# Weights and activations of a split-precision decoder step, laid out with equal addresses modulo 256 bytes

## Chip, cores and metric

The kernel runs on one core of one Trainium2 chip. The metric is the device time of one execution in microseconds; of the kernel before there are three, with a median of 1106.64 us.

## What is computed

One layer of a hybrid decoder trunk, for a prompt of 256 tokens and for 8 sequences of 4 new tokens, 288 tokens in all. `D_MODEL` is 2048, `D_FF` 8192, all arrays float32. Cut to what matters:

```python
h = rmsnorm(x, norm1_g)
proj = einsum("btd,de->bte", h, w_in) + b_in          # 2048 -> 3072
a, gate, z = split(proj)                              # 1024 each
u = a * sigmoid(gate)
c = silu(layernorm(depthwise_causal_conv(u_ext, conv_w, conv_b), ln_g, ln_b))
d = multiscale_pool(z_ext, pos0)                      # windows 2, 4, 8, 16
p = einsum("btgc,gce->btge", d, pool_w) * pool_scale
x = x + einsum("btm,md->btd", concat([c, p]), w_out)  # 2048 -> 2048
f = square(relu(einsum("btd,df->btf", rmsnorm(x, norm2_g), w_ff1)))
x = x + einsum("btf,fd->btd", f, w_ff2)
y = rmsnorm(x, norm_f)
```

## The kernel before

**Products in three parts.** Channels lie on the partitions and the 288 tokens on the free axis. A product of float32 matrices is made of three matmuls in the type float32r: every operand is split into a high part (a rounded copy) and a low part (what the rounding left), and `gemm` (L283 to L301) adds high weights by high activations (L297), high weights by low activations (L298) and low weights by high activations (L299) into one bank of PSUM. A matmul is 128 channels by 128 outputs by 288 tokens. `gemm` goes over k, the tiles of 128 input channels, and within each k over m, the two output tiles of 128; so six matmuls belong to one k. All matrices together make 8112 of them: 3072 each for `w_ff1` and `w_ff2`, 768 for `w_out`, 1152 for `w_in`, 48 for the pool weights.

**Weights.** They come in blocks of 1024 x 256 (`load`, L153), as two raw tiles of four k by 256 columns, on SP's DMA queue. `split` (L273) takes two tiles for each raw tile from the pool `wspl` (`spl`, L267: `whi` and `wlo`, five buffers of each), and `split_part` (L251) fills them in one of three ways, by the table `WAYS`: ACT always makes the high part (L257); the low part comes from DVE (way V, L262), from POOL in two halves (way G, L265), or, in way D, ACT writes the negative of the high part (L259) and a DMA on POOL's queue adds the raw weights to it (L260). The feed-forward weights all go way V. `columns` (L270) gives the slices of one k and m.

**Activations.** `act2` (L117) gives one tile for two k: `[P, 2, 2, T]`, with the low part in slot 0 and the high part in slot 1 of each k. `hx` (the first norm), `dx` (pooling), `mx` (convolution group), `ax` (second norm) and `fx` (feed-forward) are made so. For `ax`, the groups 4 and 5 lie in the place of `z_all` (L563 to L565), the groups 6 and 7 in tiles of the tag `c` (L567 to L571).

**Addresses.** A slot of an activation tile is 288 x 4 = 1152 bytes, 4.5 x 256. All tiles of weights and activations start at 128 modulo 256 bytes, and their sizes are multiples of 256. So, modulo 256: weights, high and low, are read from 128 for every k and m; high activations from 128 + 1152, that is 0; low activations from 128.

**Order.** A scheduler places the instructions of each engine by the time at which it expects them; the convolution's work is put back by `later`. The order of the groups is written out in `SEQUENCE`: eight convolution pairs and four pool groups with the first layer's weights, then eight groups of `w_out` for the pool half and eight for the convolution half, with the layer norm between them (`ln_mean`, L506), then four rounds of eight groups of `w_ff1` and eight of `w_ff2`. TensorE takes the products in this order; the scheduler can interleave neighbours.

Of the kernel before, what the change touches and what calls it, by code (L numbers as in the profile page):

```python
# [10 lines left out]
F32R = mybir.dt.float32r  # L11
AF = mybir.ActivationFunctionType
ALU = mybir.AluOpType
# [3 lines left out]
P = 128  # L17
# [3 lines left out]
T = SEQ + NB * NS  # L21
# [62 lines left out]
def trunk_kernel(ctx: ExitStack, tc: tile.TileContext, io):  # L84
# [3 lines left out]
    nc = tc.nc  # L88
# [4 lines left out]
    wspl = ctx.enter_context(tc.tile_pool(name="wspl", bufs=5))  # L93
    actp = ctx.enter_context(tc.tile_pool(name="actp", bufs=8))
# [8 lines left out]
    def nm(s):  # L103
        seen[s] = seen.get(s, 0) + 1
        return f"{s}{seen[s]}"
# [11 lines left out]
    def act2(name, **kw):  # L117

        t = actp.tile([P, 2, 2, T], F32R, name=nm(name), **(kw or {"tag": "act"}))
        return t[:, :, 1, :], t[:, :, 0, :]  # L120

    def tmp(name, n=T, tag="tmp", bufs=2):
        return tmpp.tile([P, n], F32, name=nm(name), tag=tag, bufs=bufs)
# [4 lines left out]
    def f32(t):  # L128
        return t.bitcast(F32)
# [41 lines left out]
    def by_pair(t):  # L171
        return t[:].rearrange("p (i k) c -> p i k c", i=2)
# [76 lines left out]
    turns = {}  # L249

    def split_part(raw, src, hi, lo, way):  # L251

        nc.scalar.copy(hi, raw)  # L257
        if way == "D":
            nc.scalar.activation(lo, f32(hi), AF.Copy, scale=-1.0)  # L259
            nc.gpsimd.dma_start(lo, src, accum_op=ALU.add)  # L260
        elif way == "V":
            nc.vector.tensor_tensor(lo, raw, f32(hi), op=ALU.subtract)  # L262
        else:
            for j in range(0, raw.shape[1], 2):
                nc.gpsimd.tensor_tensor(lo[:, j : j + 2, :], raw[:, j : j + 2, :], f32(hi[:, j : j + 2, :]), op=ALU.subtract)  # L265

    def spl():  # L267
        return [wspl.tile([P, 4, 256], F32R, name=nm("w" + part), tag="w" + part) for part in ("hi", "lo")]

    def columns(hi, lo, k, m):  # L270
        return hi[:, k, m * P : (m + 1) * P], lo[:, k, m * P : (m + 1) * P]

    def split(halves, stage="ff"):  # L273

        parts = []
        for raw, src in halves:
            turns[stage] = turns.get(stage, -1) + 1
            parts.append(spl())
            ways = WAYS.get(stage) or WAYS[stage[0]]
            split_part(raw, src, *parts[-1], ways[turns[stage] % len(ways)])  # L280
        return lambda k, m: columns(*parts[k // 4], k % 4, m)

    def gemm(banks, rhs, m_outer=False, between={}):  # L283
# [25 lines left out]
    def halves(x2):  # L309

        return [(x2[0][:, m, :], x2[1][:, m, :]) for m in range(2)]


    hx, firsts = [], []

    def first_split(k0, n):
        for k in range(k0, k0 + n):
            if k % 2 == 0:
                hx.extend(halves(act2("hx")))
            hh, hl = hx[k]  # L320
            nc.scalar.activation(hh, xT[:, k, :], AF.Copy, scale=v("norm1_g", k))
            nc.vector.scalar_tensor_tensor(out=hl, in0=xT[:, k, :], scalar=v("norm1_g", k), in1=f32(hh), op0=ALU.mult, op1=ALU.subtract)
        if k0 % 2 == 0:
            firsts.append([by_pair(t) for t in spl()])
        at = slice(k0 % 2, k0 % 2 + n)
        raw, hi, lo = (t[:, :, at, :] for t in (raws[k0 // 2], *firsts[k0 // 2]))
        split_part(raw, None, hi, lo, "V")
# [9 lines left out]

    def pool_weights(g):
        raw, (hi, lo) = load_pool(g), spl()
        split_part(raw[:, 0:2, :], None, hi[:, 0:2, :], lo[:, 0:2, :], "V")  # L340
        return lambda k, m: columns(hi, lo, k, m)

    def weight_groups():
# [197 lines left out]
    for j, c in enumerate(cs):  # L541
        n = tmpp.tile([P, 2, T], F32, name=nm("n"), tag="ag", bufs=2)
        nc.vector.tensor_tensor(n, c, norm["rows"][:, None, :].to_broadcast([P, 2, T]), op=ALU.mult)
        for m in range(2):
            i = 2 * j + m
# [9 lines left out]
    for g in range(8):  # L555
        bk = bank2()
        gemm(each(bk), mixc)
        x2 = xT[:, 2 * g : 2 * g + 2, :]
        nc.vector.tensor_tensor(x2, x2, bk[:, :, :T], op=ALU.add)
        if g < 4:  # L560
            a2 = halves(act2("ax", tag="p", bufs=4))
        elif g < 6:
            if g == 4:  # L563
                ax45 = zp.tile([P, N8 * ZL], F32R, name="ax45", tag="z")
                ax45 = ax45[:, 32 : 32 + 8 * T].rearrange("p (g m q t) -> p g m q t", g=2, m=2, q=2)  # L565
            a2 = halves((ax45[:, g - 4, :, 1, :], ax45[:, g - 4, :, 0, :]))
        else:  # L567
            a2 = []
            for m in range(2):
                t2 = actp.tile([P, 2, T], F32R, name=nm("ax"), tag="c", bufs=4)  # L570
                a2.append((t2[:, 1, :], t2[:, 0, :]))  # L571
        for m, (ah, al) in enumerate(a2):
            k = 2 * g + m
            xk = xT[:, k, :]
            nc.scalar.activation(ah, xk, AF.Copy, scale=v("norm2_g", k))
            nc.vector.scalar_tensor_tensor(out=al, in0=xk, scalar=v("norm2_g", k), in1=f32(ah), op0=ALU.mult, op1=ALU.subtract)
            x1.append((ah, al))
            if k == 0:
                nc.scalar.activation(ss2, xk, AF.Square)
            else:  # L580
                q2 = tmp("q")
                nc.scalar.activation(q2, xk, AF.Square)
                nc.gpsimd.tensor_tensor(ss2, ss2, q2, op=ALU.add)
# [107 lines left out]
```

## Time and profile before

| what | us |
|---|---|
| runs: median (lowest, highest) | 1106.64 (1105.6, 1106.66) |
| profiled execution: span from first to last instruction | 1103.1 |
| PE busy | 1087.3 (99%) |
| DVE busy | 638.2 (58%) |
| ACT busy | 477.8 (43%) |
| POOL busy | 179.1 (16%) |

Of the profiled execution only the span is given; the runs' median is 3.5 us above it. PE is TensorE's matmul row and PEld its weight loads, which overlap it; DVE, ACT and POOL are VectorE, ScalarE and GpSimd; SP issues most of the DMAs. Matmuls are pipelined: each takes some 290 ns from start to end, and the next starts long before that, so their rate is read from their starts. In a row of instructions the name after the line is the output tile, then the inputs, without buffer numbers.

### The profile page before, as it was taken

The page shows a single profiled execution, that of the slowest core. Times are in us where ns is not written, and L with a number is a line of the kernel's source. Part 1 is how long each engine was busy: PE and PEld are TensorE (multiplying, and loading weights), DVE is VectorE, ACT ScalarE, POOL GpSimd, SP SyncE. Part 2 cuts the span into 40 slices and gives each one's busy share as a digit, 9 for nine tenths or more (in the row PEclk, how much of TensorE's full clock was granted, in tenths as well). Part 3 has the DMA queues.
Part 4 walks back from the last instruction along what each step waited for, and adds up shares of the span by engine and source line. Part 5 has one row for each costly group of instructions (what it writes and reads, how often), then busy time and mean ns, then how long its engine had stood idle before and what let it go on. Part 6 is the DMA issues. An engine that isn't in the chain of part 4 may idle for free.

```text
span 1103.1 us, 19716 instructions
## 1 busy us (share of the span) xinstructions
PE 1087.3 (99%) x8204; PEld 1085.0 (98%) x8204; DVE 638.2 (58%) x814; ACT 477.8 (43%) x585; POOL 179.1 (16%) x209
## 2 busy tenths in 40 slices
PE   9999999999999999999999999999999999999996
PEld 8999999999999999999999999999999999999996
DVE  7889999787555444445544444545544445554553
ACT  8654445565544433333443333444433334444441
POOL 0879989512000000000000000000000000000000
PEclk9999999999999999999999999999999999999998
DMA  9996568555555555555555555555555555555522
GB/s 334 279 275 176 155 159 245 168 169 162 166 161 170 168 162 168 171 161 165 170 167 162 171 163 165 171 168 161 169 170 160 168 171 164 165 170 163 164 75 86
DMA packets 58265, 191.24 MB, mean 173 GB/s; under 512 B 6208, under 2 KB 11328, under 8 KB 58176
## 3 DMA queue, kind: packets, MB, share of 16 engines
q1 hardware_dynamic: 56752, 185.53, 53.7%
q0 software_dynamic: 1152, 4.19, 2.1%
q8 instruction: 64, 1.05, 0.4%
q10 hardware_dynamic: 272, 0.26, 0.1%
q14 instruction: 25, 0.20, 0.0%
HBM read 185.68 MB, written 4.28 MB: 172 GB/s over the span
## 4 chain that ended last, share of the span: by engine, by line
PE 89%; DVE 8%; DMA 1%; issue 1%; ACT 1%; POOL 0%; SPq 0%; DVEq 0%; POOLq 0%
PE ac L297 30%; PE ac L299 30%; PE ac L298 29%; DVE pc L415 3%; DVE wlo L262 1%; DMA wlo<-in_w 1%; DVE xT L631 0%; DMA wr<-in_w 0%; DVE c L421 0%; POOL prd L419 0%; DVE q L521 0%; DVE dx L456 0%; DVE c L515 0%; PE pt L242 0%; DVE d L449 0%
## 5 line engine op out<-in xcount | busy, mean ns | idle before, releaser
L257 ACT CAST whi<-wr 128x1024 fp32r<-128x1024 f32 (+1 forms) x341 | 355.6, 1043 | 570.8 <-PE ac L298 537.1
L262 DVE TENSOR_TENSOR wlo<-wr,whi 128x1024 fp32r<-128x1024 f32 (+1 forms) x295 | 363.1, 1231 | 353.4 <-ACT whi L257 352.3
L297 PE MATMUL ac<-ax,whi 128*128 128x288 f32 x1024 | 303.2, 296 | 0.0
L297 PE MATMUL ac<-fx,whi 128*128 128x288 f32 x1024 | 303.1, 296 | 0.0
L299 PE MATMUL ac<-ax,wlo 128*128 128x288 f32 x1024 | 301.9, 295 | 0.0
L299 PE MATMUL ac<-fx,wlo 128*128 128x288 f32 x1024 | 301.9, 295 | 0.0
L298 PE MATMUL ac<-ax,whi 128*128 128x288 f32 x1024 | 298.5, 292 | 0.0
L298 PE MATMUL ac<-fx,whi 128*128 128x288 f32 x1024 | 298.5, 292 | 0.0
L298 PEld LDWEIGHTS ac<-fx,whi 128*128 128x128 f32 x1024 | 192.5, 188 | 0.0
L298 PEld LDWEIGHTS ac<-ax,whi 128*128 128x128 f32 x1024 | 192.5, 188 | 0.0
L297 PEld LDWEIGHTS ac<-ax,whi 128*128 128x128 f32 x1024 | 192.4, 188 | 0.0
L297 PEld LDWEIGHTS ac<-fx,whi 128*128 128x128 f32 x1024 | 192.4, 188 | 0.0
L299 PEld LDWEIGHTS ac<-ax,wlo 128*128 128x128 f32 x1024 | 191.5, 187 | 0.0
L299 PEld LDWEIGHTS ac<-fx,wlo 128*128 128x128 f32 x1024 | 191.5, 187 | 0.0
L297 PE MATMUL ac<-hx,whi 128*128 128x288 f32 x384 | 113.4, 298 | 1.3 <-ACT whi L257 1.3
L299 PE MATMUL ac<-hx,wlo 128*128 128x288 f32 x384 | 110.9, 295 | 1.0 <-DMA wlo<-in_w 0.8
L298 PE MATMUL ac<-hx,whi 128*128 128x288 f32 x384 | 111.4, 292 | 0.0
L265 POOL TENSOR_TENSOR wlo<-wr,whi 128x512 fp32r<-128x512 f32 x76 | 103.8, 1413 | 37.0 <-ACT whi L257 35.5
L415 DVE SCALAR_TENSOR_TENSOR pc<-u_all,vec,pc 128x256 f32<-128x256 f32 x232 | 99.7, 481 | 3.5 <-ACT pc L412 2.3
L297 PEld LDWEIGHTS ac<-hx,whi 128*128 128x128 f32 x384 | 72.3, 189 | 1.7 <-ACT whi L257 1.7
L299 PEld LDWEIGHTS ac<-hx,wlo 128*128 128x128 f32 x384 | 71.2, 188 | 1.5 <-DMA wlo<-in_w 1.0
L298 PEld LDWEIGHTS ac<-hx,whi 128*128 128x128 f32 x384 | 72.2, 188 | 0.0
(117 smaller groups left out, 826.8 us busy)
## 6 DMA issues: line engine op xcount, KB each, us to landing
wr<-in_w SPq DMA_DIRECT2D x335, 512.0 KB, 3.8
wlo<-in_w POOLq DMA_DIRECT2D x8, 512.0 KB, 7.3
xT<-in_xT SPq DMA_DIRECT2D x7, 288.0 KB, 8.0
wr<-in_w SPq DMA_DIRECT2D x5, 256.0 KB, 3.7
out_u_out<-u_all SPq DMA_DIRECT2D x1, 1208.0 KB, 8.6
out_yT<-xT SPq DMA_DIRECT2D x2, 576.0 KB, 2.9
u_all<-in_hist_c SPq DMA_DIRECT2D x8, 136.0 KB, 5.4
out_z_out<-z_all SPq DMA_DIRECT2D x1, 668.0 KB, 9.1
```

The source lines that it names most:

```text
L257: nc.scalar.copy(hi, raw)
L262: nc.vector.tensor_tensor(lo, raw, f32(hi), op=ALU.subtract)
L265: nc.gpsimd.tensor_tensor(lo[:, j : j + 2, :], raw[:, j : j + 2, :], f32(hi[:, j : j + 2, :]), op=ALU.subtract)
L297: nc.tensor.matmul(b, wh, xh, start=k == 0, stop=False)
L298: nc.tensor.matmul(b, wh, xl, start=False, stop=False)
L299: last = nc.tensor.matmul(b, wl, xh, start=False, stop=k == n - 1)
L415: nc.vector.scalar_tensor_tensor(out=dst, in0=up[:, w : w + SEQ], scalar=cwv[:, w : w + 1], in1=pc, op0=ALU.mult, op1=ALU.add)
```

## The change

Both parts of the split weights and of the activations get a layout in which the address modulo 256 bytes depends on k alone. High and low weights share one tile `w` of 2 x 1056 elements: the row stands for k odd or even, its length of 4224 bytes is 16.5 x 256, and in each row lie 512 elements of the high part and 512 of the low part, 256 for each k. The activation tile keeps its size, and its first index now tells high from low, the second one k: two k are 1152 bytes apart, high and low 2304 (9 x 256). So, modulo 256, high and low parts of weights and activations of an even k all start at 128, those of an odd k all at 0. The other places that make or cut such tiles follow: in way D there are two DMAs of half a tile instead of one, in way G the two halves cover the same k as before, and raw weights are read in the order of the new tile.

```diff
     def act2(name, **kw):
         t = actp.tile([P, 2, 2, T], F32R, name=nm(name), **(kw or {"tag": "act"}))
-        return t[:, :, 1, :], t[:, :, 0, :]
+        return t[:, 0, :, :], t[:, 1, :, :]
...
         nc.scalar.copy(hi, raw)
         if way == "D":
             nc.scalar.activation(lo, f32(hi), AF.Copy, scale=-1.0)
-            nc.gpsimd.dma_start(lo, src, accum_op=ALU.add)
+            for i in range(2):
+                nc.gpsimd.dma_start(lo[:, i], src[:, i], accum_op=ALU.add)
         elif way == "V":
             nc.vector.tensor_tensor(lo, raw, f32(hi), op=ALU.subtract)
         else:
-            for j in range(0, raw.shape[1], 2):
-                nc.gpsimd.tensor_tensor(lo[:, j : j + 2, :], raw[:, j : j + 2, :], f32(hi[:, j : j + 2, :]), op=ALU.subtract)
+            for i in range(2):
+                nc.gpsimd.tensor_tensor(lo[:, i], raw[:, i], f32(hi[:, i]), op=ALU.subtract)
 
     def spl():
-        return [wspl.tile([P, 4, 256], F32R, name=nm("w" + part), tag="w" + part) for part in ("hi", "lo")]
+
+        t = wspl.tile([P, 2, 1056], F32R, name=nm("w"), tag="w")
+        return [t[:, :, a : a + 512].rearrange("p q (i c) -> p i q c", i=2) for a in (0, 512)]
 
     def columns(hi, lo, k, m):
-        return hi[:, k, m * P : (m + 1) * P], lo[:, k, m * P : (m + 1) * P]
+        return [t[:, k // 2, k % 2, m * P : (m + 1) * P] for t in (hi, lo)]
...
-            split_part(raw, src, *parts[-1], ways[turns[stage] % len(ways)])
+            split_part(by_pair(raw), src.rearrange("p (i k) c -> p i k c", i=2), *parts[-1], ways[turns[stage] % len(ways)])
...
-            firsts.append([by_pair(t) for t in spl()])
+            firsts.append(spl())
...
-        split_part(raw[:, 0:2, :], None, hi[:, 0:2, :], lo[:, 0:2, :], "V")
+        split_part(raw[:, 0:2, :], None, hi[:, 0, :, :], lo[:, 0, :, :], "V")
...
-                ax45 = ax45[:, 32 : 32 + 8 * T].rearrange("p (g m q t) -> p g m q t", g=2, m=2, q=2)
-            a2 = halves((ax45[:, g - 4, :, 1, :], ax45[:, g - 4, :, 0, :]))
+                ax45 = ax45[:, 32 : 32 + 8 * T].rearrange("p (g q m t) -> p g q m t", g=2, m=2, q=2)
+            a2 = halves((ax45[:, g - 4, 0], ax45[:, g - 4, 1]))
         else:
-            a2 = []
-            for m in range(2):
-                t2 = actp.tile([P, 2, T], F32R, name=nm("ax"), tag="c", bufs=4)
-                a2.append((t2[:, 1, :], t2[:, 0, :]))
+            t2 = [actp.tile([P, 2, T], F32R, name=nm("ax"), tag="c", bufs=4) for _ in range(2)]
+            a2 = [(t2[0][:, m, :], t2[1][:, m, :]) for m in range(2)]
```

## The prediction

> **What bounds the kernel now.** I read the page's first two parts, then the busy time by stretch, the waits of TensorE, and the timeline of single matmuls. The page says which engine it is:
>
> ```profile
> span 1103.1 us, 19716 instructions
> PE 1087.3 (99%) x8204; PEld 1085.0 (98%) x8204; DVE 638.2 (58%) x814; ACT 477.8 (43%) x585; POOL 179.1 (16%) x209
> ```
>
> TensorE is busy 99% of the span, and there is one weight load for each matmul. Busy time alone says little, since matmuls overlap; what matters is how far apart they start. The stretches give that (columns: stretch, its length, then busy us and number of instructions of PE, PEld, DVE, ACT and POOL, the granted clock, the DMA share, GB/s):
>
> ```profile
> 0.00:200.00 200.00, 194.88 (x1446) 193.08 (x1446) 180.80 (x359) 111.71 (x160) 156.09 (x189) 1.00 0.78 231
> 200.00:1080.00 880.00, 879.68 (x6657) 879.37 (x6658) 449.93 (x442) 363.92 (x420) 22.99 (x21) 1.00 0.52 162
> 1080.00:1104.00 24.00, 12.75 (x104) 12.56 (x102) 7.44 (x14) 2.17 (x5) 0.00 (x0) 0.82 0.25 99
> ```
>
> From 200 to 1080 us, 6657 matmuls start in 880 us without a gap, at full granted clock: one every 132.2 ns. No other engine is near its limit there (DVE 51%, ACT 41%, DMA 52%). So in this stretch every nanosecond of the pace is worth 6.7 us, and nothing else is worth anything. Before 200 us it is different: DVE is busy 180.8 of 200 us, and TensorE's waits, few as they are, name what is late:
>
> ```profile
> PE pmean L510 <- DVE sum_c L508: 1.3, 1, 1.3
> PE ac L299 <- DMA wlo<-in_w: 0.8, 1, 0.8
> ```
>
> Now single matmuls, 18 intervals from the feed-forward part (columns: start in us, duration, engine, line). L297 multiplies high weights by high activations, L298 high weights by low activations, L299 low weights by high activations:
>
> ```profile
> 600.42 0.29 PE L297 MATMUL ac<-fx,whi 128*128 128x288 f32 x1
> 600.55 0.29 PE L298 MATMUL ac<-fx,whi 128*128 128x288 f32 x1
> 600.68 0.30 PE L299 MATMUL ac<-fx,wlo 128*128 128x288 f32 x1
> 600.82 0.30 PE L297 MATMUL ac<-fx,whi 128*128 128x288 f32 x1
> 600.95 0.29 PE L298 MATMUL ac<-fx,whi 128*128 128x288 f32 x1
> 601.08 0.29 PE L299 MATMUL ac<-fx,wlo 128*128 128x288 f32 x1
> 601.21 0.29 PE L297 MATMUL ac<-fx,whi 128*128 128x288 f32 x1
> 601.35 0.29 PE L298 MATMUL ac<-fx,whi 128*128 128x288 f32 x1
> 601.48 0.30 PE L299 MATMUL ac<-fx,wlo 128*128 128x288 f32 x1
> 601.61 0.30 PE L297 MATMUL ac<-fx,whi 128*128 128x288 f32 x1
> 601.75 0.29 PE L298 MATMUL ac<-fx,whi 128*128 128x288 f32 x1
> 601.87 0.29 PE L299 MATMUL ac<-fx,wlo 128*128 128x288 f32 x1
> 602.00 0.29 PE L297 MATMUL ac<-fx,whi 128*128 128x288 f32 x1
> 602.14 0.29 PE L298 MATMUL ac<-fx,whi 128*128 128x288 f32 x1
> 602.27 0.30 PE L299 MATMUL ac<-fx,wlo 128*128 128x288 f32 x1
> 602.40 0.30 PE L297 MATMUL ac<-fx,whi 128*128 128x288 f32 x1
> 602.54 0.29 PE L298 MATMUL ac<-fx,whi 128*128 128x288 f32 x1
> 602.67 0.29 PE L299 MATMUL ac<-fx,wlo 128*128 128x288 f32 x1
> 602.80 0.29 PE L297 MATMUL ac<-fx,whi 128*128 128x288 f32 x1
> ```
>
> The whole stretch is 2.38 us for 18 intervals, 132.2 ns each. Sorted by the line that begins the interval, six of each: from L297 to L298 0.82 us, mean 136.7 ns; from L298 to L299 0.77 us, 128.3 ns; from L299 to the next L297 0.79 us, 131.7 ns. The three are equal in shape and in work, and they differ.
>
> **What runs beside what.** The weight loads in the same place:
>
> ```profile
> 600.82 0.19 PEld L298 LDWEIGHTS ac<-fx,whi 128*128 128x128 f32 x1
> 600.96 0.19 PEld L299 LDWEIGHTS ac<-fx,wlo 128*128 128x128 f32 x1
> ```
>
> The load for L298 starts with the L297 matmul (600.82), that for L299 within 10 ns of the L298 matmul (600.95). So while a matmul streams its activations, the weights of the next one are being read. By the layout, modulo 256 bytes: weights start at 128 always, high activations at 0, low ones at 128. Beside L297 and L299 the two reads differ by 128; only beside L298 are they equal, and that is the short interval. I call an interval S when operand streamed and weights loaded have the same residue (128.3 ns) and D when not ((136.7 + 131.7) / 2 = 134.2 ns). Now each three products hold one S and two D.
>
> **The change part by part.** The products, their number and their shapes stay. What moves is the residue: after it, everything of an even k starts at 128, everything of an odd k at 0 (1152 bytes further among the activations, 4224 among the weights, each 128 over a multiple of 256). Both operands of a product are alike. Beside a matmul streams the load for the next product: same k in five of six, so S; after the sixth comes the next k with the other residue, so D. The pace becomes (5 x 128.3 + 134.2) / 6 = 129.3 ns, 2.9 less than 132.2.
>
> *From 200 to 1080 us:* 6657 x 2.9 ns = 19.3 us less. What else could be late there? Splits: one ACT copy and one DVE subtraction each, ACT at 41% and DVE at 51%, and 2% less time for them leaves both far from full.
>
> *Before 200 us:* 1446 x 2.9 ns would be 4.2 us, but DVE is 90% busy and its sums of the convolution are what TensorE waits for at L510. A faster TensorE only waits longer there. I count nothing; bounds 0 to 4.2 us less.
>
> *The splits.* ACT's and DVE's operands become two blocks of two runs of 256 elements in place of one run of 1024, with as many elements. POOL's half-tiles remain two per tile. I cost these at nothing: the cover is ACT's and DVE's idle half after 200 us. If DVE's instructions grew in the first 200 us, its 90% would be the place where it shows.
>
> *The accumulating DMAs* (way D, L259 and L260) become two of half the size:
>
> ```profile
> wlo<-in_w POOLq DMA_DIRECT2D x8, 512.0 KB, 7.3
> wr<-in_w SPq DMA_DIRECT2D x5, 256.0 KB, 3.7
> L260 POOL DMA_DIRECT2D wlo<-in_w x8 | 7.9, 984 | 4.7 <-ACT wlo L259 3.2 <-ACT prd L417 1.5
> ```
>
> Eight more issues on POOL at 984 ns are 7.9 us, in a stretch where POOL is busy 156 of 200 us; what stands behind them on POOL are its own subtractions and the sample products. Two halves in place of one may land later than 7.3 us, at most by another 3.7. Each destination is in runs of 1 KB instead of 4. TensorE waits 0.8 us for one of these today. Bounds for the end: 0 to 6 us (eight waits of 0.8). I take 1, nearest to the row that exists.
>
> *High and low weights in one tile.* The ACT copy that refills a buffer may now wait for L299 rather than L298, one matmul, 0.13 us; with five buffers that is hidden.
>
> Sum: this execution took 1103.1 us of span, and the median of the runs is 3.5 above it, which I leave as it is. 1106.6 - 19.3 + 1.0 = **1088.3 us**.
>
> The Trainium skill speaks against any effect: "TensorE: Matmul & The Clock Gate" (What happens when you issue a matmul, step 1) says that TensorE has two independent read ports into SBUF, so that loading the next weights takes nothing from the running matmul; and "SBUF — State Buffer" (Who interferes with whom) says that PE and ACT never wait on anyone. By that rule the pace would not move. The same TensorE page gives a spacing of N / 2.4 + 2.5 ns, by estimate 122.5 ns for 288 columns; this trace has 132.2, so something outside the rule costs 9.7 ns, and no row says what.
>
> **Rivals.** *Slower: the lateness is at a product's own start.* The same rows can be read otherwise. L298 is the only product whose own two operands have equal residues, and it is also the one that starts late: 136.7 ns after L297, against 131.7 for the L297 that follows L299. The short interval after it may only be this lateness given back. After the change every product is of this kind. If each starts 136.7 ns after the last and nothing is given back, it is 4.5 ns more on all 1446 + 6657 matmuls, +36.5 us, 1143 us. The point from which it decides: 136.7 - 128.3 = 8.4 ns lie between all and nothing, 4.5 of them bring it to no change; when under 54% is given back, it is slower. For it speaks that an early stretch has the same products and residues without a short S:
>
> ```profile
> 32.57 0.30 PE L297 MATMUL ac<-hx,whi 128*128 128x288 f32 x1
> 32.70 0.29 PE L298 MATMUL ac<-hx,whi 128*128 128x288 f32 x1
> 32.83 0.29 PE L299 MATMUL ac<-hx,wlo 128*128 128x288 f32 x1
> 32.96 0.29 PE L297 MATMUL ac<-hx,whi 128*128 128x288 f32 x1
> 33.09 0.30 PE L298 MATMUL ac<-hx,whi 128*128 128x288 f32 x1
> 33.22 0.29 PE L299 MATMUL ac<-hx,wlo 128*128 128x288 f32 x1
> 33.35 0.29 PE L297 MATMUL ac<-hx,whi 128*128 128x288 f32 x1
> ```
>
> Six intervals of 0.13: here S is no shorter than D. The pace can settle in more than one pattern, so what a stream of equal products settles in is not in this trace. Against it: the mean there, 130 ns, is below 132.2, so intervals are not simply shifted between neighbours.
>
> *The activations alone.* L298 is also the only product whose activations start at 128. If that makes the short interval, whatever the weights, half of all products have it afterwards instead of a third: (128.3 + 134.2) / 2 = 131.25, 0.95 ns less, -6.3 us, 1101 us.
>
> *Nothing.* Residues don't matter, and the pattern is a beat of the matmul queue, as the rule above would have it. Then 132.2 stays and the DMAs' 1 us is added: 1107.6 us.
>
> **How the numbers follow.** The forecast has 43%, activations alone 12%, nothing 10%, slower 35%. A measurement of this kernel tells about 0.2%, 2.2 us, from no change, so 1104.4 to 1108.9 counts as the same. That gives faster 55%, same 10%, slower 35%. Bounds: the short interval stands as 0.12 or 0.13 in the rows; at 125 ns the pace is (5 x 125 + 134.2) / 6 = 126.5, 5.7 ns less on all 8103 matmuls, 46 us, 1061 us. The other end is 1143. The range leaves off the outermost of both: 1063 to 1140. Within it the forecast's own range is 1063 to 1101.
>
> **What would show it.** In the profile after: the number of matmuls between 200 us and 20 us from the end, over that time, is the pace; 129.3 ns is right, 132 is nothing, above 133 is the rival. The three lines should have equal intervals within a k, and the sixth should be longer. If the first and last of the six are late and the rest are short, or all are 136, the reading by the neighbouring load is wrong. If TensorE waits for the halves of the low weights by more than some 2 us in all, the term of the DMAs is wrong; if the first 200 us shrink by over 3 us, DVE was not the bound there.

## The result, and the profile after

| what | us |
|---|---|
| before, 6 runs: median (lowest, highest) | 1106.12 (1104.96, 1108.46) |
| after, 6 runs: median (lowest, highest) | 1116.72 (1113.86, 1118.06) |
| ratio, 95% interval | 1.0083 (1.0067 to 1.0100) |
| profiled execution of after: device time, span | 1114.0, 1112.2 |

The change makes the kernel slower: by 0.83% by the ratio, some 9 us, and by 10.6 us by the medians. The likeliest case of the prediction was a gain of 18 us. The profiled execution is one of the quickest of its six, so its trace shows 9.1 us of the 10.6. The page of after:

```profile
span 1112.2 us, 19636 instructions
PE 1093.0 (98%) x8204; PEld 1091.3 (98%) x8204; DVE 640.5 (58%) x814; ACT 477.3 (43%) x585; POOL 192.1 (17%) x217
```

TensorE is still the busy one, with as many matmuls. POOL has 8 instructions and 13.0 us more. The stretches of after, in the columns of the prediction (stretch, length, busy us and count of PE, PEld, DVE, ACT, POOL, then granted clock, DMA share, GB/s):

```profile
0.00:20.00 20.00, 16.34 (x94) 15.86 (x95) 13.10 (x22) 15.88 (x28) 1.72 (x33) 0.91 0.89 320
...
60.00:180.00 120.00, 117.10 (x873) 116.81 (x874) 114.24 (x235) 58.87 (x85) 116.64 (x115) 0.99 0.71 194
...
172.00:177.00 5.00, 4.64 (x23) 4.64 (x24) 4.93 (x12) 2.01 (x3) 5.00 (x6) 0.66 0.82 306
...
0.00:200.00 200.00, 192.81 (x1418) 191.81 (x1419) 178.85 (x353) 109.24 (x158) 164.42 (x193) 0.98 0.78 226
200.00:1080.00 880.00, 878.35 (x6620) 877.80 (x6618) 450.07 (x442) 363.22 (x417) 27.66 (x25) 1.00 0.51 163
...
320.00:1060.00 740.00, 740.00 (x5576) 740.00 (x5575) 354.28 (x332) 288.02 (x309) 0.00 (x0) 1.00 0.51 166
```

and four of the same stretches of before:

```profile
0.00:20.00 20.00, 17.44 (x110) 16.79 (x111) 13.68 (x23) 16.38 (x29) 1.73 (x33) 1.00 0.90 319
60.00:180.00 120.00, 119.50 (x902) 119.04 (x901) 114.93 (x240) 61.87 (x88) 107.50 (x112) 1.00 0.71 194
...
172.00:177.00 5.00, 4.83 (x36) 4.84 (x37) 4.15 (x12) 4.09 (x6) 5.00 (x6) 1.00 0.80 248
...
320.00:1060.00 740.00, 740.00 (x5599) 740.00 (x5598) 355.49 (x334) 289.16 (x311) 0.00 (x0) 1.00 0.53 166
```

Three things can be read here. From 200 to 1080 us 6620 matmuls start where before had 6657: the pace became slower, not faster. The 37 missing ones are 4.9 us at 132.2 ns; 1.3 of these are TensorE idle (878.35 busy against 879.68; it is the wait for the sums ahead of the layer norm, which in before lies just ahead of 200 us), and 3.6 are pace. From 60 to 180 us 29 fewer start, TensorE is busy 2.4 us less, and POOL is now busy for 116.6 of 120 us where it was for 107.5. Part of this loss is the clock: from 172 to 177 us it is 0.66 where before has 1.00, and 23 matmuls start instead of 36. In the first 20 us 16 fewer start, at a granted clock of 0.91.

The start of the matmul with the same number in both traces gives the sum in time order: after is 2.1 us late by the 98th matmul (18 us in before), 3.1 by the 400th (59 us), 5.2 by the 1400th (192 us) and 9.1 by the last. So 2.1 us are lost at the start, 3.1 from there to 200 us, and 3.9 behind it. TensorE's waits in after (us, times, longest):

```profile
PE ac L300 <- ACT w L257: 2.4, 1, 2.4
PE ac L302 <- POOL w L266: 1.8, 1, 1.8
PE ac L302 <- DMA w<-in_w: 1.7, 1, 1.7
PE pmean L513 <- DVE sum_c L511: 1.4, 1, 1.4
```

The first is 1.3 us in before. The second is new, low weights that POOL makes too late; the third, for those of an accumulating DMA, has doubled from 0.8. Behind the second, at 172 us, 14 matmuls start 240 ns apart before the usual pace comes back; they cost another 1.5 us. POOL's issues of these DMAs, in before and in after (a timeline of POOL: start, duration, line; x2 is two in a row) show why:

```profile
67.10 0.83 POOL L260 DMA_DIRECT2D wlo<-in_w  x1
```

```profile
70.29 2.42 POOL L261 DMA_DIRECT2D w<-in_w  x2 [0.42 <-POOL w L266]
```

```profile
q0 software_dynamic: 4352, 4.20, 2.5%
...
w<-in_w POOLq DMA_DIRECT2D x16, 256.0 KB, 8.5
```

One tile cost POOL 0.83 us, its two halves cost 2.42; eight tiles make that 12.7 us, about the 13.0 that POOL has more. The queue moves as many bytes in 4352 packets, where the page of before has 1152, and they land 8.5 us after the issue instead of 7.3. (The mean of single POOL records is no guide here: behind such an issue the records of the next instructions overlap it.)

Single matmuls of after (L300 high by high, L301 high weights by low activations, L302 low weights by high activations), one k:

```profile
601.07 0.29 PE L300 MATMUL ac<-fx,w 128*128 128x288 f32 x1
601.20 0.29 PE L301 MATMUL ac<-fx,w 128*128 128x288 f32 x1
601.33 0.30 PE L302 MATMUL ac<-fx,w 128*128 128x288 f32 x1
601.47 0.29 PE L300 MATMUL ac<-fx,w 128*128 128x288 f32 x1
601.60 0.30 PE L301 MATMUL ac<-fx,w 128*128 128x288 f32 x1
601.74 0.29 PE L302 MATMUL ac<-fx,w 128*128 128x288 f32 x1
601.87 0.29 PE L300 MATMUL ac<-fx,w 128*128 128x288 f32 x1
```

Six intervals in 0.80 us: 133 ns, none of them as short as 128. The starts in the trace are finer than these rows. By them the six intervals of a k have means of 132.5, 135.9, 132.5, 130.9, 130.0 and 135.0 ns from 320 to 1060 us; the first five were to be 128.3. In before the same six positions have 137.5, 125.8, 131.7, 133.3, 132.5 and 132.5 ns.

The pace is best read where POOL is idle, from 320 to 1060 us: the length over the number of matmuls. Before has 740 us / 5599 = 132.2 ns; the number for every kernel is given below in this way.

### The profile page after: what moved, and what is told of

It reads as the page before. It is cut to its first block, busy times and chain, and to the rows that moved or that the text cites. A ratio compares the mean times of both kernels' runs of the same rounds, so it can differ in the third digit from the quotient of the medians.

```text
span 1112.2 us, 19636 instructions
## 1 busy us (share of the span) xinstructions
PE 1093.0 (98%) x8204; PEld 1091.3 (98%) x8204; DVE 640.5 (58%) x814; ACT 477.3 (43%) x585; POOL 192.1 (17%) x217
## 3 DMA queue, kind: packets, MB, share of 16 engines
q0 software_dynamic: 4352, 4.20, 2.5%
## 4 chain that ended last, share of the span: by engine, by line
PE 85%; POOL 6%; DVE 3%; issue 2%; DMA 2%; ACT 1%; SPq 0%; DVEq 0%; POOLq 0%; ACTq 0%
PE ac L301 28%; PE ac L302 28%; PE ac L300 28%; POOL w L266 3%; POOL s L447 1%; DVE pc L418 1%; DMA w<-in_w 1%; POOL prd L422 1%; DVE w L263 1%; ACT w L257 1%; DMA xT<-in_xT 0%; DMA wr<-in_w 0%; DVE xT L632 0%; POOL s L455 0%; POOL d L456 0%
## 5 line engine op out<-in xcount | busy, mean ns | idle before, releaser
L257 ACT CAST w<-wr 128x1024 fp32r<-128x1024 f32 (+1 forms) x341 | 355.1, 1042 | 573.1 <-PE ac L302 551.8
L263 DVE TENSOR_TENSOR w<-wr,w 128x1024 fp32r<-128x1024 f32 (+1 forms) x295 | 364.9, 1237 | 364.8 <-ACT w L257 364.5
L301 PE MATMUL ac<-fx,w 128*128 128x288 f32 x1024 | 303.1, 296 | 0.0
L301 PE MATMUL ac<-ax,w 128*128 128x288 f32 x1024 | 303.1, 296 | 0.0
L302 PE MATMUL ac<-fx,w 128*128 128x288 f32 x1024 | 302.6, 296 | 0.0
L302 PE MATMUL ac<-ax,w 128*128 128x288 f32 x1024 | 302.6, 295 | 0.0
L300 PE MATMUL ac<-ax,w 128*128 128x288 f32 x1024 | 301.7, 295 | 0.0
L300 PE MATMUL ac<-fx,w 128*128 128x288 f32 x1024 | 301.6, 295 | 0.0
L300 PEld LDWEIGHTS ac<-fx,w 128*128 128x128 f32 x1024 | 193.9, 189 | 0.0
L300 PEld LDWEIGHTS ac<-ax,w 128*128 128x128 f32 x1024 | 193.9, 189 | 0.0
L302 PEld LDWEIGHTS ac<-fx,w 128*128 128x128 f32 x1024 | 192.5, 188 | 0.0
L302 PEld LDWEIGHTS ac<-ax,w 128*128 128x128 f32 x1024 | 192.5, 188 | 0.0
L301 PEld LDWEIGHTS ac<-ax,w 128*128 128x128 f32 x1024 | 192.0, 188 | 0.0
L301 PEld LDWEIGHTS ac<-fx,w 128*128 128x128 f32 x1024 | 192.0, 188 | 0.0
L266 POOL TENSOR_TENSOR w<-wr,w 128x512 fp32r<-128x512 f32 x76 | 113.8, 1688 | 32.8 <-ACT w L257 32.1
L300 PE MATMUL ac<-hx,w 128*128 128x288 f32 x384 | 112.5, 296 | 2.4 <-ACT w L257 2.4
L302 PE MATMUL ac<-hx,w 128*128 128x288 f32 x384 | 111.4, 298 | 1.9 <-DMA w<-in_w 1.7
L301 PE MATMUL ac<-hx,w 128*128 128x288 f32 x384 | 112.7, 296 | 0.0
L300 PEld LDWEIGHTS ac<-hx,w 128*128 128x128 f32 x384 | 72.9, 191 | 2.7 <-ACT w L257 2.7
L302 PEld LDWEIGHTS ac<-hx,w 128*128 128x128 f32 x384 | 72.0, 190 | 2.4 <-DMA w<-in_w 1.9
L301 PEld LDWEIGHTS ac<-hx,w 128*128 128x128 f32 x384 | 72.4, 189 | 0.0
```

The lines of the kernel that those rows point to most:

```text
L266: nc.gpsimd.tensor_tensor(lo[:, i], raw[:, i], f32(hi[:, i]), op=ALU.subtract)
L300: nc.tensor.matmul(b, wh, xh, start=k == 0, stop=False)
L301: nc.tensor.matmul(b, wh, xl, start=False, stop=False)
L302: last = nc.tensor.matmul(b, wl, xh, start=False, stop=k == n - 1)
```

## Experiments

Theory, after the result: the pace is set by the addresses of both the product's own operands and the next load, the first 200 us by the cost of the shorter runs. Rivals: the pace follows the product's own equality alone; or it is the layout, not the residues, that costs.

**e1: the layout without the residues.** After, with the weight tile at 1024 elements per row and the activations as before, so the residues are those of before:

```diff
-        t = wspl.tile([P, 2, 1056], F32R, name=nm("w"), tag="w")
+        t = wspl.tile([P, 2, 1024], F32R, name=nm("w"), tag="w")
...
-        return t[:, 0, :, :], t[:, 1, :, :]
+        return t[:, :, 1, :], t[:, :, 0, :]
```

(and likewise for `ax`.)

> The changed kernel's tiles, halved accumulating DMAs and strided splits, but with the residues of the kernel before: the rows of the weight tile are 1024 elements instead of 1056, so all weights start at 128 modulo 256, and the activations keep the old order (high at 0, low at 128). Theory A (the equal residues cost, through the pace): pace back at 132.2 ns per matmul, time within 2 us of the kernel before. Theory B (the layout costs, through waits of TensorE in the first 200 us): the pace is 132.2, yet some 5 us of the 9 stay, about 1111. Both shares can hold: the changed trace is 9.1 us behind, of which 5.5 us had come by 200 us and 3.6 us afterwards by pace; then this run is slower by about 5.

Measured: 1110.23 us, 1.0037 of before (1.0021 to 1.0053), so some 4 us, against 1.0083 for the whole change. Stretches of e1:

```profile
60.00:180.00 120.00, 117.69 (x875) 117.06 (x875) 112.82 (x232) 59.65 (x86) 116.48 (x116) 0.99 0.72 192
320.00:1060.00 740.00, 740.00 (x5599) 740.00 (x5598) 356.95 (x336) 290.04 (x313) 0.00 (x0) 1.00 0.54 166
```

The pace is that of before to the last matmul (5599), and POOL is as full as in after. By equal numbers of matmuls, e1 has lost 1.3 us at the 500th, 4.1 at the 1300th and 4.0 at the end. What follows: the layout costs about 4 us, all by the 1300th matmul (179 us in before); the slower pace comes from the residues.

**e2: every product's operands 128 apart.** After, with the weights moved by 32 elements:

```diff
-        return [t[:, :, a : a + 512].rearrange("p q (i c) -> p i q c", i=2) for a in (0, 512)]
+        return [t[:, :, a : a + 512].rearrange("p q (i c) -> p i q c", i=2) for a in (32, 544)]
```

> As the changed kernel, but the weights lie 128 bytes further in their tile, so that the two operands of every product differ by 128 modulo 256. Theory A (equal residues make a product slow): from a third of products equal (132.16 ns) and all equal (132.7 ns) a straight line gives 131.9 ns for none, 7 us less than the changed kernel. Theory B (the pace is a pattern into which equal products settle, whatever the residue): 132.7 ns as in the changed kernel, same time within 2 us. The reading of the prediction (equal is fast when load and stream meet) gives 134 ns, 9 us more than the changed kernel.

Measured: 1116.27 us, 1.0085 (1.0067 to 1.0104): the same as after. Its steady stretch:

```profile
320.00:1060.00 740.00, 740.00 (x5575) 740.00 (x5574) 354.11 (x331) 288.80 (x309) 0.00 (x0) 1.00 0.54 166
```

5575 against the 5576 of after, 132.7 ns. Whether all products have equal operands or all have different ones made no difference between these two builds. The six intervals of a k have 133.3, 136.7, 126.7, 134.2, 132.5 and 133.3 ns. Stream and next load are equal here only beside the sixth (133.3), and the one short interval (126.7) is one that the prediction calls D.

**e3: two of three products equal.** Before, with the slots of the activations swapped, so that the high ones have the residue of the weights:

```diff
-        return t[:, :, 1, :], t[:, :, 0, :]
+        return t[:, :, 0, :], t[:, :, 1, :]
```

(and likewise for `ax`.)

> The kernel before with high and low activations in the opposite slots: two of three products have equal residues instead of one of three, and nothing else changes, neither tiles nor DMAs. Theory A: 132.4 ns, 2 us slower than before. Theory B: 132.2 ns, no change. The reading of the prediction: two short intervals for one, 130.2 ns, 13 us faster.

Measured: 1105.8 us, 0.9998 (0.9989 to 1.0007), 5599 matmuls in the 740 us as before. Two S in place of one would by the prediction's prices be 130.3 ns. So these prices don't add.

**m1: streams of matmuls alone.** A kernel that only runs float32r matmuls of 288 columns, 288 to a stream, with the addresses of one pattern (its outputs are filler):

```python
for r in range(reps):
    for i, (w, x) in enumerate(products):
        nc.tensor.matmul(banks[:, i // 3 % 2, :n], ws[:, w : w + 128], xs[:, x : x + n], ...)
```

> No part of the reference is computed: matmuls of 128 x 128 x 288 follow each other without any wait, from weights and activations that stay in place, 288 in each of 18 arrangements of the residues, and the outputs are filled with constants. a and b have the order of the kernel before and of the changed one; c and d have all operands equal, e and f all different by 128, g, h, i the weights 64, 192 and 32 further, j high first, k different with alternating k; l, m, n, o are c with 256, 320, 512 and 128 columns; p and q read one and the same weights and activations, equal and different; r shifts activations by 16 bytes. Theory A: a 132.2, b 132.7, c and d 132.7 or more, e and f 131.9 or less. Theory B: all of 288 columns lie between 131 and 133, and c equals e. The reading of the prediction: c and d 128 or less, e and f 134. If the columns set the pace, l, m, n are 13 ns shorter, 13 ns longer and 93 ns longer than c; if the load of 128 weights does, l equals c.

Measured, from the starts (in m1 to m3 without the first intervals of a stream, which a rising clock or a matmul ahead can lengthen): addresses of before 132.2 ns, of after 131.7, all equal 131.7, all 128 apart 133.3. All 128 apart with the residues changing from k to k, as in e2, gives 132.8, and high activations equal (as e3) 132.2. One and the same weights and activations throughout give 131.7 when equal and 133.3 when 128 apart. Weights 32 or 64 above 133.3, 64 below 131.7, 16 below 131.7. Rows of m1 (after the count: min, median, max ns, first and last start); b is after, c all equal, e all different, k as e2, o has 128 columns:

```profile
L139 PE MATMUL ob<-xs,ws x288: 288/295/299, 49.9 to 87.6; 128*128 128x288 f32 x144
L139 PE MATMUL oc<-xs,ws x288: 292/294/296, 87.8 to 125.6; 128*128 128x288 f32 x144
L139 PE MATMUL oe<-xs,ws x288: 292/294/297, 163.6 to 201.9; 128*128 128x288 f32 x144
L139 PE MATMUL ok<-xs,ws x288: 290/295/300, 393.2 to 431.3; 128*128 128x288 f32 x144
L139 PE MATMUL oo<-xs,ws x144: 220/275/280, 502.5 to 518.4; 128*128 128x128 f32 x144
```

37.8 us over 287 intervals is 131.7 for c, 38.3 is 133.4 for e, 38.1 is 132.8 for k, 15.9 over 143 is 111 for o. What follows: residues do act, but all equal and all different lie 1.7 ns apart, not the 5.9 of the prediction's S and D; and alone, the addresses of after are *faster* than those of before, by half a nanosecond. The kernel did the opposite. With 256, 320 and 512 columns the interval is 120.0, 146.7 and 226.7 ns, 0.417 ns a column, so from 256 columns on the columns set it. At 128 columns that line would give 66.7 ns, and 111 are measured; that the weight load no longer hides there is likely, but no run shows it.

**d1: the halved DMAs alone.** Before, with each accumulating DMA cut in two, each of runs of 1 KB as in after:

```diff
-            nc.gpsimd.dma_start(lo, src, accum_op=ALU.add)
+            for i in range(2):
+                nc.gpsimd.dma_start(lo[:, i::2], src[:, i::2], accum_op=ALU.add)
```

> The kernel before, with its tiles and residues, but each accumulating DMA of way D is issued as two, over every second k, so that every run is 1 KB, as in the changed kernel. If these DMAs are what the layout costs (16 issues kept POOL busy for 27.0 us in the changed kernel, 8 for 7.9 us before), POOL is full between 60 and 180 us and the time is some 3.5 us above the kernel before, as with the layout alone. If the strided splits or the common tile of high and low weights cost it, nothing changes here: within 1 us.

Measured: 1109.54 us, 1.0036 (1.0024 to 1.0047): the whole cost of e1, with nothing else of the layout. The page's first row of d1, a pair of its DMAs, its stretch from 60 us and the waits of TensorE:

```profile
PE 1089.3 (98%) x8204; PEld 1085.8 (98%) x8204; DVE 641.5 (58%) x814; ACT 477.8 (43%) x585; POOL 192.2 (17%) x217
...
68.44 2.42 POOL L261 DMA_DIRECT2D wlo<-in_w  x2 [0.32 <-POOL wlo L266]
...
60.00:180.00 120.00, 117.66 (x885) 116.79 (x884) 114.17 (x234) 60.72 (x87) 116.65 (x115) 1.00 0.72 193
...
PE pmean L511 <- DVE sum_c L509: 2.8, 1, 2.8
PE ac L300 <- DMA wlo<-in_w: 1.8, 3, 1.2
...
PE ac L300 <- POOL wlo L266: 1.7, 1, 1.7
```

POOL's total, the 2.42 us of a pair and the full 60 to 180 us are those of after. What is late is the same: low weights from the DMAs (1.8 us) and from POOL (1.7), and here the sums ahead of the layer norm too (2.8, where before has 1.3). The last one need not belong to the DMAs, as f1 shows below. By equal numbers of matmuls d1 is 3.6 us late ahead of it. A pair of halves in long runs was not tried, so the number of DMAs and the length of their runs are not told apart.

**f1 and f2: one more matmul.** Before (f1) and after (f2) with one small matmul more, early in the feed-forward part, behind the rows of the second norm (cut: the lines that name `rows_done`):

```diff
+                side = ms("side")
+                with tc.issue_after(rows_done.ins):
+                    nc.tensor.matmul(side[:, 0, 0:64], x1[0][0][:, 0:P], x1[0][0][:, 0:64], start=True, stop=True)
```

> The kernel before with one matmul of 64 columns more, 24 products behind the rows of the second norm; its result goes nowhere. Theory P (the pace is a pattern that the stream keeps until something shifts its phase: the kernel before shows 131.1 ns between 289 and 294 us and 132.2 ns from 297 us on, with the same residues): the pattern may change, and if it falls into the one of 131.1 ns, 1.1 ns x 5900 = 6.5 us less. Rival R (the residues alone set the pace): 132.2 ns and no change, at most the 0.1 us that the matmul takes.

> The changed kernel with the same additional matmul of 64 columns. Theory P: it may leave the pattern of 132.8 ns for the one of 131.7 ns, which the changed kernel shows between 187 and 200 us: 6.5 us less than the changed kernel, about 1110. Rival R: 132.8 ns, as the changed kernel. Both: TensorE waits at about 8 us as in the changed kernel, if that belongs to the layout, or does not, if it was chance.

Measured: f1 1105.35 us, 1.0001 (0.9989 to 1.0012), 5599 matmuls in 740 us. In its profiled execution, the slowest of its ten, TensorE waits longer for the sums ahead of the layer norm than in before (1.3 us), although the added matmul comes behind them:

```profile
PE pmean L510 <- DVE sum_c L508: 2.8, 1, 2.8
```

So this wait differs from one execution to the next. f2 1107.44 us, 1.0022 (1.0009 to 1.0035), where after stands at 1.0083: 0.6%, some 7 us, are gained by *adding* a matmul. Its steady stretch:

```profile
320.00:1060.00 740.00, 740.00 (x5623) 740.00 (x5622) 358.09 (x337) 290.98 (x315) 0.00 (x0) 1.00 0.54 167
```

5623 matmuls, 131.6 ns, with every address of after. What follows: with these addresses the stream has two paces, 131.7 and 132.8 ns, and which of them it holds depends on how it was entered. 1.1 ns on 6620 matmuls are 7.3 us. The trace of after has both: 131.6 ns from 76 to 95 and from 187 to 200 us, and 132.8 from 300 us on.

**m2: phase and neighbour.** Streams as in m1, each behind nothing or behind another small matmul; and streams of single residues, among them two that take the prediction's two readings apart:

```python
"own": ("z", [(0, 0), (32, 32)] * 6),    # own operands equal, the load beside the stream differs
"next": ("z", [(32, 0), (0, 32)] * 6),   # own operands differ, the load beside the stream is equal
```

> No part of the reference is computed: 144 matmuls of 128 x 128 x 288 in a row for each arrangement, from operands that stay in place, outputs filled with constants. Arrangements a (order and residues of the kernel before), b (of the changed kernel, with its distances) and c (all equal) come six times each: with nothing between it and the one before (z), or behind a matmul of 64 (v), 128 (y) or 288 columns (h), or behind three float32 matmuls as in the sums (t) or the rows (u) of a norm. Theory P: the same arrangement runs at different paces, by what stands ahead: a at 131.1 or 132.2, b at 131.7 or 132.8 ns. Rival R: one pace for each arrangement. Then own (every product equal, the next load different) and next (every product different, the next load equal): if what a product reads itself counts, own is 131.7 and next 133.3; if what is read side by side counts, the other way round. Then weights 32, 96, 112 and 128 bytes below the activations (da, db, dc, dg) and 16, 4 and 96 above (dd, de, df): by the earlier table 131.7 below and 133.3 above.

Measured: addresses of before 132.2 ns behind nothing, a 64- or a 128-column matmul, 131.1 behind one of 288 columns. Of after 131.7 behind nothing, 132.8 behind any of these three. Behind the three float32 matmuls of a norm's sums they have 131.1 and 131.7, behind those of its rows 132.2 and 132.8. All equal 131.7 in all cases. "own" 134.4, "next" 129.9. Weights 112 below the activations (stream dc) 130.0, 96 below 131.7, 32 or 128 below 133.3, 4 or 96 above 133.3, 16 above 132.0; so the rule expected, 131.7 below and 133.3 above, does not hold.

```profile
L151 PE MATMUL oown<-xs,ws x144: 292/297/300, 358.7 to 377.9; 128*128 128x288 f32 x144
L151 PE MATMUL onext<-xs,ws x144: 288/292/297, 378.0 to 396.6; 128*128 128x288 f32 x144
L151 PE MATMUL odc<-xs,ws x144: 290/291/293, 434.9 to 453.5; 128*128 128x288 f32 x144
```

143 intervals in 19.2 and 18.6 us: 134.3 and 130.1 by the rows. What follows: against a stream with neither equality (133.3), an equal load beside the stream saves 3.4 ns, and a product's own equality seems to cost 1.1. With both, 131.7 ns. So both readings of the prediction may be true at once, and a layout that makes *everything* equal buys the gain and pays it back in part. But "own" and "next" ran once each, behind nothing, and what runs ahead moves some of the streams above by 1.1 ns and one of m3 by 2.2. The 3.4 is clear of that, the 1.1 is not.

**m3: a scan of the distance.** Addresses of before and of after, with the weights moved up in 16 steps of 16 bytes (streams a to p), each twice, behind nothing and behind a 64-column matmul.

> No part of the reference is computed: 120 matmuls of 128 x 128 x 288 for each arrangement, outputs filled with constants. The order of the kernel before (a) and that of the changed one (b), each with all weights moved by 0 to 240 bytes in steps of 16 (last letter a to p), once behind nothing (z) and once behind one matmul of 64 columns (v). Theory L (a product waits for what the load read beside the stream reads, so the pace depends on the distance between weights and activations, beside the phase): b at a distance of 16 below minus 96 (last letter j, 144 bytes) runs at 130 ns, as it did with 112 bytes below, a and i at 131.7 or 132.8 and 133.3. Theory P alone (only the phase): the 16 distances of one order differ by no more than z and v of one distance do. For a no distance beats 130 ns, and equal and different products both stand in it, so 130.5 to 133.3 is expected.

Measured: with the activations of after, 130.6 to 133.9 ns. Step 9 (stream j), at which 130 were expected by the distance alone, runs at 132.8 behind either prelude, so that expectation failed; the last step has 132.8 behind nothing and 130.6 behind the small matmul. With the activations of before, 130.0 to 135.6 ns. The lowest is step 15, weights 112 above the high and 16 below the low activations modulo 256: 130.0 both times.

```profile
L138 PE MATMUL oazb<-xs,ws x120: 290/298/300, 28.0 to 44.1; 128*128 128x288 f32 x120
L138 PE MATMUL oazp<-xs,ws x120: 289/292/295, 251.6 to 267.1; 128*128 128x288 f32 x120
L138 PE MATMUL oavp<-xs,ws x120: 289/292/377, 763.4 to 779.0; 128*128 128x288 f32 x120
L138 PE MATMUL obzj<-xs,ws x120: 290/296/301, 410.4 to 426.2; 128*128 128x288 f32 x120
```

Step 1 (oazb) 16.1 us over 119 intervals, 135.3; step 15 (oazp) 15.5, 130.3; obzj 15.8, 132.8. Equality as such is no optimum, and a distance is good or bad only together with the order of the addresses.

**g1 and g2: that distance in the kernel, with a ring.** Before, its weight tiles cut by hand from one buffer, 16 bytes lower (g1) or at the distance of before (g2); the line that makes the buffer `ring` and two sizes that go with it are left out:

```diff
-        return [wspl.tile([P, 4, 256], F32R, name=nm("w" + part), tag="w" + part) for part in ("hi", "lo")]
+        n = turns["spl"] = turns.get("spl", -1) + 1
+        return [ring[:, 4 + 1024 * j : 4 + 1024 * (j + 1)].rearrange("p (k c) -> p k c", k=4) for j in (n % 5, 5 + n % 5)]
```

g2 has 8 for 4. In both, blocks of the first layer's weights are overwritten in another order, so the values are not the reference's; the amount of work is.

> The kernel before with all split weights 16 bytes lower against the activations, so that they start at 112 above the high activations and 16 below the low ones, modulo 256; in the scan this distance ran at 130.0 ns behind either prelude, the distance of the kernel before at 132.2. The ten weight buffers are cut from one tile in turn, since single tiles cannot be placed by 16 bytes. Theory L (the distance of the two operands of a stream sets its pace, beside the phase): 130.0 ns, 2.2 ns x 6657 = 14.7 us less from 200 us on, nothing certain before that, since VectorE and GpSimd are nearly full there: 1089 to 1092 us. Theory P alone: the stream stays at 132.2 or goes to 131.1 by its phase, 0 to 7 us less. Rival (other engines' accesses, absent in the scan, break the pattern): no change.

> The same ring of weight buffers at the distance of the kernel before (128 and 0): a control for the ring and for what moved with it. 132.2 ns and no change, within 1 us of the kernel before.

Measured: g1 1107.71 us, 1.0019 (1.0009 to 1.0028); g2 1122.9, 1.0153 (1.0137 to 1.0169). The ring makes TensorE wait 13.8 and 12.9 us at the start, so neither shows the gain against before; between the two it is 15.2 us. Paces 130.0 (5695 in 740 us) and 132.2 (5599): 2.2 ns on 6657 matmuls are 14.6.

**g3 and g4: that distance without the ring.** High and low weights in one tile of the pool, at the lower distance (g3) or at that of before (g4):

```diff
-        return [wspl.tile([P, 4, 256], F32R, name=nm("w" + part), tag="w" + part) for part in ("hi", "lo")]
+        t = wspl.tile([P, 2112], F32R, name=nm("w"), tag="w")
+        return [t[:, a : a + 1024].rearrange("p (k c) -> p k c", k=4) for a in (60, 1084)]
```

g4 has `(0, 1024)`.

> The kernel before, with high and low weights in one tile of 2112 elements (33 x 256 bytes), 240 bytes into it, so that they start 112 bytes above the high activations and 16 below the low ones, modulo 256; DMAs, splits and activations as before. Theory L (the distance sets the pace): 130.0 ns, 14.7 us less than the kernel before from 200 us on and up to 3 us before that: 1088 to 1092. Theory P (only the phase): 132.2 or 131.1 ns, 1099 to 1106.

> The control: the same common tile, but at the distance of the kernel before. 132.2 ns and no change within 1 us, if neither the common tile nor its size costs anything; 2 us more, with a granted clock of 0.91 in the first 20 us, if the late start of the changed kernel goes with the tile's size and the addresses behind it.

Measured: **g3 1095.63 us, 0.9892 of before (0.9872 to 0.9911)**, the fastest of all, 11 us under before and 21 under after. g4 1110.41, 1.0030 (1.0016 to 1.0045). The steady stretch and a wait of g3:

```profile
320.00:1060.00 740.00, 740.00 (x5694) 740.00 (x5694) 363.45 (x344) 296.11 (x321) 0.00 (x0) 1.00 0.54 167
```

```profile
PE pmean L511 <- DVE sum_c L509: 5.4, 1, 5.4
```

and of g4:

```profile
320.00:1060.00 740.00, 740.00 (x5599) 740.00 (x5598) 357.14 (x336) 290.37 (x314) 0.00 (x0) 1.00 0.53 166
```

```profile
PE pmean L511 <- DVE sum_c L509: 5.2, 1, 5.2
```

130.0 against 132.2 ns with the same tile, 14.8 us between the two, the place of the weights in it changed by 16 bytes modulo 256. In their profiled executions both wait some 4 us longer than before for the sums ahead of the layer norm (5.4 and 5.2 against 1.3), which is about what g4 loses (3.5 us by the medians). That the common tile causes this wait is likely, since it is all that g4 changes; how is not shown, and the wait varies by itself (2.8 in f1).

## Why the prediction was wrong

*The bound: right.* TensorE set the end. Three pairs of kernels show that a nanosecond of pace is worth 6.7 us: g3 and g4 (2.2 ns, 14.8 us), g1 and g2 (2.2 ns, 15.2 us), f2 and after (1.1 ns, 0.61%, 6.7 us).

*"I call an interval S when operand streamed and weights loaded have the same residue (128.3 ns) and D when not (134.2 ns)": this is the step that failed.* It gave each interval a price by one pair of residues and added these prices up for another order, to 129.3 ns. The measured pace is 132.7 in the kernel and 131.7 to 132.8 in m2's streams, and the five intervals of after that were to be S take 130.0 to 135.9 ns. The price of S was a mean over two output tiles that have the same residues and not the same intervals: in before, the one behind L298 takes 125.8 ns in the first and 132.5 in the second, as long as the D behind L299 (131.7 and 132.5). (By the starts in the trace, the six S of the rows shown have a mean of 129.2 ns; 128.3 comes from rows rounded to 10 ns.) And each price was read off one interval of a sequence in which the next one can catch up, so only the sum over a whole period could be carried over. e3 has twice as many S and the same period; in e2 the short interval is a D. What the short interval is made of is argued, not shown: by m2, L298 could start late since its own operands are equal, and the next product make it up, since the load beside it is equal, but the second output tile has the same residues and shows neither. Of the signs that the prediction named, 132.7 ns lies between "nothing" (132) and the rival (above 133).

*The rival "the lateness is at a product's own start": half right, and its price far off.* Own equality may cost (134.4 against 133.3 in m2), as it said, and the pace did go up. But nearly all is given back: 0.5 ns are left of the 4.5 it counted, and 1143 us was never near. *"The activations alone"* falls: with weights and activations both moved by 128, or only one, m1 has equal streams at 131.7 (c and d) and different ones at 133.3 (e and f), whatever the activations' own residue. *"Nothing"* comes closest in size for the pace, and is wrong all the same: a change of 16 bytes moves it by 2.2 ns (g3).

*"The pace can settle in more than one pattern": right, and under-used.* It stood as an argument for the slower rival; it is why the sign could not be had from residues at all. The same addresses run at 131.7 or 132.8 ns (f2, m2). At 131.7, after would have gained 0.5 ns, 3.5 us, and the layout would have taken them back: f2 stands at 1.0022.

*The accumulating DMAs: the mechanism named, the size wrong.* I took 1 us, within 0 to 6; d1 measures 4.0 by its ratio (2.7 to 5.2). The halves were priced at the 984 ns of whole tiles; in runs of 1 KB each took some 1.2 us for half the bytes, where a whole tile took 0.83, so POOL got 13 us more work and not 7.9, while from 60 to 180 us it had 12.5 us to spare. The end was taken to see one wait of the size in the trace; in that stretch POOL, with 3.4 of 120 us left, has no cover for its own subtractions behind the issues, and their products wait too. The sign named for this term, over 2 us of waits for the halves, did not appear (1.7 us): the loss came by POOL's own low weights (1.8 us) and by the slower clock behind that wait (1.5). The prediction had named the shorter runs and POOL's 156 of 200 us and costed neither.

*The splits and the common tile: nothing to see in the steady stretch*, as said (DVE 354 and ACT 288 of 740 us, 355 and 289 before). The common tile alone was not free where it was tried on the old order: g4 loses 3.5 us, by its trace at the layer norm. After has no such wait (1.4 us), so there the term was right.

*Before 200 us "I count nothing": no gain indeed,* but 5.2 us of loss: 3.1 by POOL and the clock, as above, and 2.1 in the first 20 us. Of the latter, TensorE's wait for the first weights (2.4 us), and behind it matmuls at intervals of 240 ns, show in the trace of after:

```profile
11.12 0.40 PE L300 MATMUL ac<-hx,w 128*128 128x288 f32 x1 [2.42 <-ACT w L257]
...
14.23 0.44 PE L301 MATMUL ac<-hx,w 128*128 128x288 f32 x1
14.47 0.44 PE L302 MATMUL ac<-hx,w 128*128 128x288 f32 x1
```

The granted clock of 0.91 in this stretch stands in after, e2, f2 and g3, and 1.00 in before, e1, e3, d1, f1 and g4, one profiled execution each. The length of the wait does not tell the groups apart; before and f2 have the same:

```profile
PE ac L297 <- ACT whi L257: 1.3, 1, 1.3
```

```profile
PE ac L300 <- ACT w L257: 1.3, 1, 1.3
```

What makes the clock go down in the one group and not in the other is **open**, and so is whether the layout has a part in it; no experiment here was made for it.

In sum for the profiled execution: 3.1 us where POOL is full (with the slower clock at 173 us), 2.1 at the start, 3.6 by the pace, and 0.3 of the 9.1 not assigned. Which of its two paces a build of after takes is shown to depend on what runs ahead (f2); what exactly sets it, and why 16 bytes matter, is open too.

## What to carry to other kernels

Two intervals of a pipelined engine are not two prices: carry over the mean of a whole period, or measure the new order by itself, before a pattern of single intervals is made a rule for the layout. When a DMA is cut up, look at the number of its pieces and at the engine that issues it, not at its bytes alone. Where one engine is bound by a steady stream, moving an operand by a few bytes is a cheap experiment (here 1.3% between g4 and g3), to be tried in the kernel itself, since the pattern that it settles in depends on what runs ahead.

## What was not expected of the hardware

- **The pace of equal matmuls depends on where their operands lie**, from 130.0 to 135.6 ns for 288 columns (m3), at full granted clock. By the rule of the Trainium skill that the prediction set against this change ("SBUF — State Buffer", Who interferes with whom) no distance would matter; here the longest pace is 4% over the shortest. That it is TensorE's two reads that collide is the nearest reading; no run shows the reads themselves.
- **One stream of the same addresses has more than one steady pace**, 131.7 or 132.8 ns with those of after, held for hundreds of microseconds (f2 and after); 131.1 or 132.2 with those of before, in streams of 19 us (m2).
- **The fixed part of an interval is large.** 120.0, 131.7, 146.7 and 226.7 ns for 256, 288, 320 and 512 columns are 12 to 13 ns over the 0.417 ns that each column adds, and at 128 columns with a load for each it stays at 111 (m1). The 2.5 ns that the prediction quotes from the Trainium skill are not seen in these float32r matmuls that each load their weights. Nor are the figures that the Trainium skill gives for such a stream ("TensorE: Matmul & The Clock Gate", Back-to-back issue gap): some 81 ns for 128 columns and 131 for 512.
- **A wait of TensorE can cost more than itself.** Behind a wait of 1.8 us the matmuls of after start 240 ns apart for 3 us, at a granted clock of 0.66 from 172 to 177 us, and lose 1.5 us more. Behind d1's 1.7 us for the same weights the clock stays at 1.00 (60 to 180 us).
- **An accumulating DMA of half the bytes cost POOL more than a whole one**: 0.83 us for 128 runs of 4 KB, 1.2 us for 256 runs of 1 KB (before, d1, after).
